# A gate multiplication two products later and two split remainders: moving VectorE work around a held gate-up pair

## The chip, the core and the metric

The kernel runs on one core of a Trainium2 chip. The metric is the device time of one execution in microseconds (us). Engines are named as the profile names them: PE is TensorE's matmul, PEld its weight load, DVE is VectorE, ACT is ScalarE, POOL is GpSimd, SP is SyncE, which issues DMAs.

## What is computed

A two-layer streaming encoder over 576 tokens (512 of a prompt and 64 of a sample) with width 1024. Each layer has two half-step SwiGLU feed-forward blocks (FFN), a mixer and a cross attention, each with a residual add. Only the FFN matters here:

```python
def swiglu(x, w_gu, w_down):
    gate, up = jnp.split(x @ w_gu, 2, axis=-1)
    return (jax.nn.silu(gate) * up) @ w_down
...
x = x + 0.5 * swiglu(rms_norm(x, ln_ffn1[l]), w_ffn1_gu[l], w_ffn1_down[l])
```

The hidden width is 2816, which is 22 tiles of 128. All values are fp32. A float32 product is made of three matmuls on rounded parts (high times high, high times low, low times high), so every operand needs a high part and a remainder.

## The kernel before

**Pairs and products.** Three of the four FFNs (the last one of layer 0 and both of layer 1) multiply by a scheme with seven products in place of eight. A *pair* is two weight tiles, gate and up of one hidden tile, or two output tiles of the down projection. Its seven products are numbered k = 0 to 6; `PLACE` says which of the three PSUM banks T, Y, W of the pair each goes to (k = 0, 3, 4, 6 to T, 1 and 5 to Y, 2 to W). Consecutive pairs alternate between two sets of banks. A product into a bank can start only when the epilogue of the product before it in that bank has been read out.

**Weights.** A weight piece arrives by DMA in `wraw` or `raw`. ACT casts it to the high part `wh` (`hi`, L149) and DVE subtracts to get the remainder `wl` (`lo`, L155). Both are made in program order about two to four products ahead of use. A sum of two pieces (`ss`, L319) is made by DVE and added to another piece by a DMA that POOL issues.

**Order of the work.** The program is a list of steps, one for each product. For each step the code first prepares weights (casts and remainders), then emits the matmuls, then calls the epilogue `pair_epi` (gate-up) or `down_epi` (down), and then `tick`, which runs what `defer(fn, n)` has put off: a function deferred by n in the epilogue of one step runs after the step n later. Each engine executes its own instructions in the order in which they were emitted.

**Parts and held pairs.** The 22 hidden tiles are worked in four parts of 6, 6, 4 and 6. Between the gate-up pairs of one part and its four down pairs D, E, ... stands one gate-up pair H of the next part. It is the *held* pair (`jj == 0 and not first`): its split hidden tile is kept back until the down pairs are done. There are three such places in each of the three FFNs, nine in all. The pair before H, the last gate-up pair of the part, is called G. Around the place the products run in this order:

```
... D.k0  H.k5  H.k4  D.k2  D.k1  H.k6  D.k3  E.k2  D.k5  D.k4 ...
```

The DVE epilogues are: H.k5, `ta` gets the second half of the gate (L599), then `gate` multiplies all of `ta` by the norm factor R (L594), and ACT's `silu` (L597) is put off; H.k4, `tc` from bank T (L610), which must be read before H.k6 may write T; H.k6, hidden = up times `ta` (L627 to L629, and L638 at six of the nine places); every down product, one L676 that adds its bank to X. D.k4 goes to the bank that the L676 of D.k3 reads. G's hidden tile is split into three operands: ACT makes the high parts, and `rest` makes the remainders: `hl<-td`, `qel<-hk` and a half-size `hl<-hk`. In the first two places of an FFN the down pairs work on six hidden tiles and their weight pieces are 384 wide (six *wide* places); in the third they work on four tiles and pieces are 256 wide (three *narrow* places).

Of the kernel before, what the change touches and what calls it, by code (L numbers as in the profile page):

```python
# [86 lines left out]
class Kernel:  # L87
# [471 lines left out]
    def ffn(self, gu, dn, gain_next, pairs=True, early=False):  # L559
# [4 lines left out]
        def pair_epi(k, pr, first, last, direct, early, late):  # L564

            T, Y, W = pr.banks
            tt = V.tensor_tensor
            jj = pr.jj
            one, two = slice(0, HF), slice(HF, NT)
            if k in (0, 2):  # L570
                if not pr.begun:
                    pr.begun = True
                    if first:
                        self.operand(st)
                        st["hk"] = self.fs["x"].tile([128, 3, HF], F32, tag="hk", name="hk")
                        for n in ("qeh", "qel"):
                            st[n] = self.fs["x"].tile([128, 2, 3, HF], F32R, tag=n, name=n)
                    pr.tb, pr.ta, pr.tc = (self.tmp(n) for n in ("tb", "ta", "tc"))
                    self.hi(pr.tb[:, one], (T, None, W)[k])
                else:  # L580
                    tt(pr.ta[:, one], (T, None, W)[k], pr.tb[:, one], op=ALU.add)  # L581
                    if last:
                        tt(pr.ta[:, one], pr.ta[:, one], st["R"][:, one], op=ALU.mult)
            elif k == 1:
                self.hi(pr.tb[:, two], Y)
            elif k == 3:
                self.hi(pr.tc[:, one], T)
                if first:
                    st["r"] = self.stats_tok(self.acc, self.ones, 1.0, ps=self.banks[:, 6:8])
                elif "R" not in st:  # L590
                    st["dg"] = self.diag(st["r"], "td")
            elif k == 5:
                def gate(c=slice(0, NT)):
                    tt(pr.ta[:, c], pr.ta[:, c], st["R"][:, c], op=ALU.mult)  # L594

                def silu():
                    nc.scalar.activation(pr.ta, pr.ta, AF.Silu)  # L597

                tt(pr.ta[:, two], Y, pr.tc[:, one], op=ALU.add)  # L599
                if first:  # L600
                    st["R"] = self.stats_bcast(None, dg=st.pop("dg"), ps=self.banks[:, 6:8])
                if last:
                    gate(two)
                    silu()
                    gate()
                else:
                    gate()
                    self.defer(silu, 3)
            elif k == 4:
                tt(pr.tc[:, two], T, pr.tb[:, two], op=ALU.add)  # L610
            else:
                qh, ql = st["qhh"], st["qhl"]
                kk = jj // 2
                hk = st["hk"]
                if direct or jj % 2:
                    h = self.tmp("td")
                else:
                    h = hk[:, 1:3].rearrange("p c n -> p (c n)")
                if last:
                    hh, hl = st["hh"][:, jj], st["hl"][:, jj]  # L620
                    for c, x in ((one, T), (two, pr.tc[:, two])):
                        tt(h[:, c], x, pr.ta[:, c], op=ALU.mult)
                        self.hi(hh[:, c], h[:, c])
                    for c in (one, two):
                        self.lo(hl[:, c], h[:, c], hh[:, c])
                    return
                tt(h[:, one], T, pr.ta[:, one], op=ALU.mult)  # L627
                tt(h[:, two], pr.tc[:, two], pr.ta[:, two], op=ALU.mult)
                tt(h, h, st["R"], op=ALU.mult)  # L629
                def sums():  # L630
                    tt(hk[:, 2], h[:, two], hk[:, 2], op=ALU.subtract)
                    V.scalar_tensor_tensor(hk[:, 1], hk[:, 2], -1.0, hk[:, 1], op0=ALU.mult, op1=ALU.subtract)
                    V.scalar_tensor_tensor(hk[:, 0], h[:, one], -1.0, hk[:, 1], op0=ALU.mult, op1=ALU.subtract)

                if direct:
                    parts = [(st["hh"][:, jj], st["hl"][:, jj], h)]
                elif jj % 2 == 0:
                    tt(hk[:, 0], hk[:, 1], hk[:, 2], op=ALU.subtract)  # L638
                    parts = [(qh[:, 0:2, kk], ql[:, 0:2, kk], hk[:, 0:2])]
                else:  # L640
                    parts = [(qh[:, 2:4, kk], ql[:, 2:4, kk], self.h2(h)),
                             (st["qeh"][:, :, kk], st["qel"][:, :, kk], hk[:, 1:3]),
                             (qh[:, 4, kk], ql[:, 4, kk], hk[:, 0])]

                def rest(ps):
                    for oh, ol, x in ps:
                        self.lo(ol, x, oh)

                def tail():
                    for oh, ol, x in parts:  # L650
                        self.hi(oh, x)
                    n = 0 if early or direct and late else 1
                    self.defer(lambda: rest(parts[:1]), n)
                    if parts[1:]:
                        self.defer(lambda: rest(parts[1:]), n + 1)

                if jj == 0 and not first:
                    st["held"] = tail
                elif direct and late:
                    tail()  # L660
                elif direct or jj % 2 == 0:
                    self.defer(tail, 1)
                elif early:
                    sums()
                    self.defer(tail, 1)
                else:
                    self.defer(lambda: (sums(), self.defer(tail, 0)), 1)
# [17 lines left out]
        def gate_up(j, jj, nj, direct):  # L685
            pr = Pair(gu[2 * j], gu[2 * j + 1],
                      lambda k, pr: pair_epi(k, pr, j == 0, direct and jj == nj - 1, direct, j == 0 or jj == nj - 1, jj == nj - 2), ops)
            pr.jj, pr.begun = jj, False
            seq.append(pr)
# [8 lines left out]
        parts = PARTS_S if pairs else PARTS  # L698
# [1813 lines left out]
```

## Time and profile before

| | before |
|---|---|
| device time, median of 3 runs | 2508.59 us (2506.38 to 2508.71) |
| the profiled execution, its own time | 2503.67 us |
| its span from first to last instruction | 2501.8 us |
| mean granted TensorE clock | 0.993 |
| PE busy | 2435.1 us, 97% |
| DVE busy | 1811.8 us, 72% |
| ACT busy | 1147.2 us, 46% |

The span lies 1.9 us inside the execution's own time, and that execution was 4.9 us faster than the median. Busy shares are means over the whole span: DVE at 72% has stretches in which it never rests. In a row of the trace, the part in brackets is how long the engine sat idle before the instruction and what ended that.

### The profile page before, as it was taken

What the parts mean: (1) busy time and instruction counts of PE and PEld (TensorE: products, weight loads), DVE (VectorE), ACT (ScalarE), POOL (GpSimd) and SP (SyncE); (2) the same over time, 40 slices, a digit from 0 to 9 for tenths busy, and PEclk for the clock granted to TensorE, in tenths of its full rate; (3) what the DMA queues carried; (4) which work ended last, traced back from release to release, by engine and by line L of the source; (5) the groups of instructions that cost most, each with busy time, mean ns of one, the idle gap of its engine ahead of it and who ended that gap; (6) DMA issues with size and microseconds to landing.
All of it is one profiled execution on the core that took longest, in us unless ns stands there. A gap on an engine that the chain in (4) does not pass through costs nothing.

```text
span 2501.8 us, 46574 instructions
## 1 busy us (share of the span) xinstructions
PE 2435.1 (97%) x18211; PEld 2391.6 (96%) x18211; DVE 1811.8 (72%) x3329; ACT 1147.2 (46%) x2093; POOL 617.3 (25%) x775
## 2 busy tenths in 40 slices
PE   8999999999999999999999999999999999999998
PEld 8998999999899999999999999999999999999998
DVE  6645658667875589898888888876753468989885
ACT  5222222334655465455556454452452355544554
POOL 1576135302320012222202222212310001222221
PEclk9999999999999999999999999999999999999999
DMA  4365653321134446766646767755972225676662
GB/s 157 91 189 186 154 129 116 120 96 37 37 107 134 131 118 148 169 156 160 150 112 147 169 142 179 158 148 174 295 250 86 84 94 135 144 181 150 155 144 76
DMA packets 160093, 350.87 MB, mean 140 GB/s; under 512 B 21585, under 2 KB 64257, under 8 KB 159233
## 3 DMA queue, kind: packets, MB, share of 16 engines
q1 hardware_dynamic: 115808, 277.09, 34.4%
q0 software_dynamic: 44064, 70.80, 18.1%
q8 instruction: 144, 2.36, 0.4%
q14 instruction: 77, 0.62, 0.1%
HBM read 292.26 MB, written 31.97 MB: 130 GB/s over the span
## 4 chain that ended last, share of the span: by engine, by line
PE 72%; DVE 12%; DMA 6%; ACT 3%; POOL 3%; issue 3%; SPq 1%; ACTq 0%; DVEq 0%; POOLq 0%
PE banks L349 34%; PE banks L428 27%; PE banks L2027 2%; DVE wl L236 2%; PE banks L772 1%; PE banks L1408 1%; PE banks L1376 1%; PE banks L1923 1%; PE banks L2303 1%; DVE wl L155 1%; DMA b<-in_ssm_bw 1%; ACT wh L149 1%; DMA f<-s5f 1%; DMA wraw<-ss 1%; DVE hl L155 1%
## 5 line engine op out<-in xcount | busy, mean ns | idle before, releaser
L149 ACT ACTIVATE wh<-wraw 128x512 fp32r<-128x512 f32 (+3 forms) x627 | 440.7, 719 | 339.6 <-PE banks L349 113.8
L236 DVE TENSOR_TENSOR wl<-wraw,wh 128x1024 fp32r<-128x1024 f32 (+2 forms) x216 | 262.5, 1220 | 153.3 <-ACT wh L149 151.0
L349 PE MATMUL banks<-xh,wh 128*128 128x288 f32 x1056 | 311.8, 295 | 1.6 <-ACT wh L149 1.3
L349 PE MATMUL banks<-xh,wl 128*128 128x288 f32 x1056 | 312.2, 296 | 1.0 <-DVE wl L155 0.9
L349 PE MATMUL banks<-xl,wh 128*128 128x288 f32 x1056 | 311.7, 295 | 0.0
L155 DVE TENSOR_TENSOR wl<-wraw,wh 128x512 fp32r<-128x512 f32 (+2 forms) x396 | 246.0, 627 | 59.3 <-ACT wh L149 58.2
L428 PE MATMUL banks<-xh,wh 128*128 128x288 f32 x1232 | 267.8, 299 | 9.0 <-ACT wh L149 8.1
L428 PE MATMUL banks<-xh,wl 128*128 128x288 f32 x1232 | 265.6, 297 | 4.2 <-DVE wl L236 4.2
L428 PE MATMUL banks<-xl,wh 128*128 128x288 f32 x1232 | 264.5, 297 | 0.0
L349 PE MATMUL banks<-eh,wh 128*128 128x288 f32 x792 | 236.9, 299 | 21.0 <-DVE tc L610 18.4
L349 PE MATMUL banks<-el,wh 128*128 128x288 f32 x792 | 234.5, 296 | 0.0
L349 PE MATMUL banks<-eh,wl 128*128 128x288 f32 x792 | 234.4, 296 | 0.0
L428 PE MATMUL banks<-hh,wh 128*128 128x288 f32 x1032 | 222.8, 297 | 3.6 <-ACT hh L149 1.8
L428 PE MATMUL banks<-hh,wl 128*128 128x288 f32 x1032 | 221.6, 296 | 3.3 <-DVE wl L236 3.3
L428 PE MATMUL banks<-hl,wh 128*128 128x288 f32 x1032 | 221.5, 296 | 0.5 <-DVE hl L155 0.5
L428 PEld LDWEIGHTS banks<-xh,wh 128*128 128x128 f32 x1232 | 199.5, 190 | 11.2 <-ACT wh L149 8.6
L428 PEld LDWEIGHTS banks<-xh,wl 128*128 128x128 f32 x1232 | 199.2, 190 | 5.5 <-DVE wl L236 5.4
L323 POOL DMA_DIRECT2D wraw<-ss x96 | 84.2, 885 | 473.8 <-DVE ta L581 217.7
L349 PEld LDWEIGHTS banks<-xh,wh 128*128 128x128 f32 x1056 | 199.0, 188 | 2.1 <-ACT wh L149 1.5
L349 PEld LDWEIGHTS banks<-xh,wl 128*128 128x128 f32 x1056 | 198.7, 188 | 1.5 <-DVE wl L155 1.5
L428 PEld LDWEIGHTS banks<-xl,wh 128*128 128x128 f32 x1232 | 199.4, 190 | 0.0
L349 PEld LDWEIGHTS banks<-xl,wh 128*128 128x128 f32 x1056 | 198.7, 188 | 0.0
(568 smaller groups left out, 6242.4 us busy)
## 6 DMA issues: line engine op xcount, KB each, us to landing
wraw<-in_gu SPq DMA_DIRECT2D x110, 512.0 KB
raw<-in_gu SPq DMA_DIRECT2D x66, 512.0 KB
wraw<-in_dn SPq DMA_DIRECT2D x56, 384.0 KB
raw<-in_gu POOLq DMA_DIRECT2D x66, 256.0 KB, 5.9
wraw<-in_gu POOLq DMA_DIRECT2D x66, 256.0 KB, 4.5
wraw<-ss POOLq DMA_DIRECT2D x66, 256.0 KB, 3.5
raw<-in_dn SPq DMA_DIRECT2D x24, 384.0 KB
wraw<-in_win SPq DMA_DIRECT2D x17, 512.0 KB
```

What stands on the lines that cost most here:

```text
L149: self.nc.scalar.activation(out, in_, AF.Copy)
L155: self.nc.vector.tensor_tensor(out, in_, hi.bitcast(F32), op=ALU.subtract)
L236: self.lo_engine.tensor_tensor(l[:p, :n], t[:p, :n], h[:p, :n].bitcast(F32), op=ALU.subtract)
L323: self.nc.gpsimd.dma_start(pr.r1[:, two], pr.src[3], accum_op=ALU.add)
L349: mm(out, ww[:, ws], xx[:, kk], start=k < 3 and kk == 0 and pi == 0, stop=kk == kn - 1 and pi == 2, skip_group_check=True)
L428: mm(ps[:M, h, :n], ww[:, k * M:(k + 1) * M], xx[:, k0 + k, h * n:(h + 1) * n], start=first and k == 0 and pi == 0, stop=last and k == kt ...
L772: nc.tensor.matmul(ps, ww[:, k * 128:(k + 1) * 128], xx[:, k, c0:c0 + n], start=k == 0 and pi == 0, stop=k == nj - 1 and pi == 2)
L1376: mm(out, x[:, k, t * 128:t * 128 + m], y[:, k], start=k == 0 and pi == 0, stop=k == 1 and pi == 2)
L1408: mm(out, x[:, k, f * 128:(f + 1) * 128], y[:, k, ts], start=k == 0 and pi == 0, stop=k == 1 and pi == 2)
L1923: mm(pv[:, m], x[:, kk, ms], y[:, k * MEM:(k + 1) * MEM], start=kk == m == pi == 0, stop=kk == 7 and pi == 2 and m == 1)
L2027: mm(ps[:, h, :HF], ww[:, k * 128:(k + 1) * 128], xx[:, k, h * HF:(h + 1) * HF], start=k == 0 and pi == 0, stop=k == 7 and pi == 2)
L2303: self.nc.tensor.matmul(out, ww[:, k * 128:(k + 1) * 128], xx[:, k], start=k == 0 and pi == 0, stop=k == KT - 1 and pi == 2)
```

## The change

For the held pair, `gate` is no longer emitted in the epilogue of H.k5: `gate` and `silu` together are deferred by two steps, so `gate` comes after D.k2 in place of H.k5 and `silu` after D.k2 in place of D.k1. For G (`early and not first`, with three operands), the second and third remainders come one and three products later.

```diff
                     gate(two)
                     silu()
                     gate()
+                elif jj == 0 and not first:
+                    self.defer(lambda: (gate(), silu()), 2)
                 else:
                     gate()
                     self.defer(silu, 3)
@@
                     for oh, ol, x in parts:
                         self.hi(oh, x)
                     n = 0 if early or direct and late else 1
-                    self.defer(lambda: rest(parts[:1]), n)
-                    if parts[1:]:
-                        self.defer(lambda: rest(parts[1:]), n + 1)
+                    for i, p in enumerate(parts):
+                        self.defer(lambda p=p: rest([p]), n + ((0, 2, 4) if early and not first else (0, 1, 1))[i])
```

The order of instructions changes on DVE and ACT alone; POOL's and SP's rows stay as they were but for buffer numbers. In the changed file the lines from 606 on move down by one or two: L610 becomes L612, L627 becomes L629, L676 becomes L677.

On DVE, at the first wide place, from behind L599 to H.k6's first epilogue instruction, before:

```order
L594 TENSOR_TENSOR ta<-ta,R 128x576
L155 TENSOR_TENSOR qel<-hk,qeh 128x2x288
L155 TENSOR_TENSOR hl<-hk,hh 128x288
L155 TENSOR_TENSOR wl<-ss,wh 128x384
L610 TENSOR_TENSOR tc<-banks,tb 128x288
L155 TENSOR_TENSOR wl<-wraw,wh 128x384
L319 TENSOR_TENSOR ss<-raw_10744,wraw 128x384
L676 SCALAR_TENSOR_TENSOR X<-banks,X 128x288
L155 TENSOR_TENSOR wl<-wraw,wh 128x384
L676 SCALAR_TENSOR_TENSOR X<-banks,X 128x288
L155 TENSOR_TENSOR wl<-wraw,wh 128x384
L627 TENSOR_TENSOR hk<-banks,ta 128x288
```

The same stretch in the changed kernel:

```order
L155 TENSOR_TENSOR wl<-ss,wh 128x384
L612 TENSOR_TENSOR tc<-banks,tb 128x288
L155 TENSOR_TENSOR qel<-hk,qeh 128x2x288
L155 TENSOR_TENSOR wl<-wraw,wh 128x384
L319 TENSOR_TENSOR ss<-raw_10744,wraw 128x384
L677 SCALAR_TENSOR_TENSOR X<-banks,X 128x288
L594 TENSOR_TENSOR ta<-ta,R 128x576
L155 TENSOR_TENSOR wl<-wraw,wh 128x384
L677 SCALAR_TENSOR_TENSOR X<-banks,X 128x288
L155 TENSOR_TENSOR hl<-hk,hh 128x288
L155 TENSOR_TENSOR wl<-wraw,wh 128x384
L629 TENSOR_TENSOR hk<-banks,ta 128x288
```

The same twelve instructions stand in both; `gate` (L594) and the two remainders have moved from ahead of H.k4's read-out to behind it. The three `wl<-wraw` rows are called A, B and C in what follows.

On ACT, at the same place, from the cast of the summed piece on, before:

```order
L149 ACTIVATE wh<-ss 128x384
L149 ACTIVATE wh<-wraw 128x384 x2
L597 ACTIVATE ta<-ta 128x576
L149 ACTIVATE wh<-wraw 128x384 x2
L149 ACTIVATE wh<-raw_10744 128x384
```

The same stretch in the changed kernel:

```order
L149 ACTIVATE wh<-ss 128x384
L149 ACTIVATE wh<-wraw 128x384
L597 ACTIVATE ta<-ta 128x576
L149 ACTIVATE wh<-wraw 128x384 x3
L149 ACTIVATE wh<-raw_10744 128x384
```

`silu` (L597) has moved ahead of one cast, the one for piece B; casts B and C now both stand behind it, and cast A stays ahead of it. At the narrow places it stands ahead of the casts of B and C in the same way.

## Rows read from the trace of the kernel before

**Rows 1.** The page, busy time of each engine over the span.

```profile
PE 2435.1 (97%) x18211; PEld 2391.6 (96%) x18211; DVE 1811.8 (72%) x3329; ACT 1147.2 (46%) x2093; POOL 617.3 (25%) x775
```

**Rows 2.** PE's waits: who waited <- for whom: us in total, times, longest.

```profile
PE banks L349 <- DVE tc L610: 18.4, 12, 2.3
```

**Rows 3.** Timeline of PE, first wide place: start, duration, what, [idle before].

```profile
1001.08 0.37 PE L349 MATMUL banks<-eh,wh 128*128 128x288 f32 x1 [1.55 <-DVE tc L610]
...
1006.08 0.29 PE L349 MATMUL banks<-hl,wh 128*128 128x288 f32 x1
1006.22 0.29 PE L349 MATMUL banks<-hh,wl 128*128 128x288 f32 x1
1006.53 0.38 PE L349 MATMUL banks<-qeh,wh 128*128 128x288 f32 x1
```

**Rows 4.** Timeline of DVE, first wide place.

```profile
997.82 0.45 DVE L599 TENSOR_TENSOR ta<-banks,tc 128x288 f32<-128x288 f32 x1
998.30 0.76 DVE L594 TENSOR_TENSOR ta<-ta,R 128x576 f32<-128x576 f32 x1
998.98 0.75 DVE L155 TENSOR_TENSOR qel<-hk,qeh 128x576 fp32r<-128x576 f32 x1
999.65 0.45 DVE L155 TENSOR_TENSOR hl<-hk,hh 128x288 fp32r<-128x288 f32 x1
1000.02 0.55 DVE L155 TENSOR_TENSOR wl<-ss,wh 128x384 fp32r<-128x384 f32 x1
1000.49 0.45 DVE L610 TENSOR_TENSOR tc<-banks,tb 128x288 f32<-128x288 f32 x1
1000.86 0.54 DVE L155 TENSOR_TENSOR wl<-wraw,wh 128x384 fp32r<-128x384 f32 x1
...
1001.79 0.44 DVE L676 SCALAR_TENSOR_TENSOR X<-banks,X 128x288 f32<-128x288 f32 x1
1002.16 0.54 DVE L155 TENSOR_TENSOR wl<-wraw,wh 128x384 fp32r<-128x384 f32 x1
...
1003.46 0.45 DVE L627 TENSOR_TENSOR hk<-banks,ta 128x288 f32<-128x288 f32 x1
...
1005.94 0.45 DVE L676 SCALAR_TENSOR_TENSOR X<-banks,X 128x288 f32<-128x288 f32 x1
```

**Rows 5.** Timeline of ACT, first wide place: casts B and C, with silu.

```profile
998.65 0.53 ACT L149 ACTIVATE wh<-wraw 128x384 fp32r<-128x384 f32 x1 [1.62 <-DMA wraw<-ss]
999.10 0.68 ACT L597 ACTIVATE ta<-ta 128x576 f32<-128x576 f32 x1
999.69 0.51 ACT L149 ACTIVATE wh<-wraw 128x384 fp32r<-128x384 f32 x1
```

**Rows 6.** Timeline of DVE, first narrow place.

```profile
1180.67 0.45 DVE L599 TENSOR_TENSOR ta<-banks,tc 128x288 f32<-128x288 f32 x1
...
1182.86 0.42 DVE L155 TENSOR_TENSOR wl<-ss,wh 128x256 fp32r<-128x256 f32 x1
1183.20 0.45 DVE L610 TENSOR_TENSOR tc<-banks,tb 128x288 f32<-128x288 f32 x1
...
1186.37 0.46 DVE L627 TENSOR_TENSOR td<-banks,ta 128x288 f32<-128x288 f32 x1 [0.66 <-PE banks L349]
...
1188.23 0.45 DVE L676 SCALAR_TENSOR_TENSOR X<-banks,X 128x288 f32<-128x288 f32 x1
```

**Rows 7.** Timelines of ACT and PE, first narrow place: cast C; H.k6.

```profile
1182.53 0.40 ACT L149 ACTIVATE wh<-wraw 128x256 fp32r<-128x256 f32 x1
1183.79 0.37 PE L349 MATMUL banks<-eh,wh 128*128 128x288 f32 x1 [2.26 <-DVE tc L610]
```

**Rows 8.** Windows H.k6 to D.k4, narrow places: span, engines' busy, granted clock, DMA.

```profile
1183.79:1189.38 5.59, 5.59 (x31) 5.59 (x31) 4.90 (x14) 1.45 (x4) 2.43 (x3) 0.69 0.34 47
1577.55:1581.88 4.33, 4.21 (x30) 4.00 (x31) 4.30 (x12) 1.45 (x4) 1.88 (x3) 1.00 0.35 45
2365.13:2370.72 5.59, 5.59 (x31) 5.59 (x31) 4.64 (x13) 1.45 (x4) 2.17 (x3) 0.69 0.33 47
```

## The prediction

> **What bounds the kernel now.** I read the page's busy times first: PE is busy for 97% of the span [rows 1], so a change is worth what it does to PE's waits. The list of PE's waits has one large entry inside the pair FFNs: twelve waits on H.k4's read-out L610, 18.4 us together [rows 2]. The timeline puts nine of them at H.k6 of the held pairs: six of about 1.55 us at the wide places, of which one stands in [rows 3], and three of about 2.27 us at the narrow ones, of which one stands in [rows 7]. That is 6 x 1.55 + 3 x 2.27 = 16.1 us, and what the change aims at. The other three, which share the remaining 2.3 us (0.77 each), belong to the last gate-up pair of each FFN, which it does not touch.
>
> Next I read what DVE does around such a wait [rows 4]. Behind L599 come the gate, `qel`, `hl`, a remainder, and only then L610. From L599 to the last row shown, the L676 that empties D.k3's bank, no row has a bracket: DVE does not rest for 8.12 us (997.82 to 1005.94). Then look at D.k4 in [rows 3]. Matmuls follow each other by about 0.13 us (1006.08, 1006.22), so D.k4 could have started at 1006.35. It started at 1006.53, when that L676 (1005.94, 0.45 long) had just ended. So at a wide place PE is held a second time, 5.45 us after the first, by the same unbroken DVE queue. What the place costs is set by when that L676 comes, not by L610.
>
> **The moved work on DVE.** The gate, `qel` and `hl` took 998.30 to 1000.02, 1.72 us, ahead of L610. They now come behind it. Nothing is added or removed: between L599 and L627 stand the same twelve instructions. From [rows 4], by distance between starts: a half-size operation such as L676 0.37 (1001.79 to 1002.16), gate 0.68, `qel` 0.67, a 384-wide remainder 0.47 (1000.02 to 1000.49), A and the sum behind it together 0.93 (1000.86 to 1001.79). The walk in the new order from L599 at 997.82: `wl<-ss` 998.19, L610 998.66, `qel` 999.03, A 999.70, L676 1000.63, gate 1001.00. L610 is 1.83 us earlier, more than PE's 1.55 us wait, so that wait closes. (L599 had 0.48 behind it because the gate reads what it writes; now 0.37, which is 0.1 gained.)
>
> If DVE kept going, remainder B would start at 1001.68, L627 at 1003.36 and the deciding L676 at 1005.84, 0.1 before its old time. PE would come to D.k4 early and wait there. The 1.55 us would be given back in full.
>
> **The moved work on ACT.** DVE does not keep going. `silu` needs the gate's result, and it now stands ahead of casts B and C. In before the gate ended at 999.06 and silu started at 999.10 [rows 4, 5]; now the gate ends at 1001.76, so silu starts at 1001.80. The next ACT instruction follows 0.59 after (999.10 to 999.69), so cast B, which ran at 998.65 in before, runs from 1002.39 to about 1002.90. Remainder B subtracts that cast; with the same 0.04 it starts at 1002.94 in place of 1001.68. DVE idles 1.26 us in a stretch that had no slack. Behind B are queued L676 of D.k1, `hl`, C, L627 to L638, and the deciding L676. On from 1002.94: L676 1003.41, `hl` 1003.78, C 1004.15 (its cast has ended by 1003.33), L627 1004.62 instead of 1003.46. From there the rows are unchanged: the deciding L676 at 1007.10, D.k4 at 1007.69. **A wide place ends 1.15 us later than before, six of them 6.9 us.**
>
> [...]
>
> **The narrow places.** The same walk with 256-wide pieces, whose remainder (and, I take it, sum) takes 0.34 (1182.86 to 1183.20), from L599 at 1180.67 [rows 6]: L610 1181.38, so H.k6 starts at 1181.97, 0.59 behind it as before (1183.20 to 1183.79); its wait falls from 2.26 to 0.44 us. `qel` 1181.75, A 1182.42, L676 1183.10, gate 1183.47 to 1184.23, silu 1184.27, cast B 1184.86 to 1185.26 (0.40 long [rows 7]), B 1185.30, L676 1185.64, `hl` 1186.01, C 1186.38, L627 1186.72 (before 1186.37, where DVE had waited 0.66 us for PE), the deciding L676 1.86 later at 1188.58, D.k4 at 1189.17 against 1189.38. That is 0.2 us gained. At the second narrow place PE was faster in before: D.k4 came 4.33 us after H.k6, not 5.59 [rows 8]. With the same distance from L599 to H.k6, the walk loses 5.59 - 4.33 - 0.2 = 1.05 us there; the third place is like the first. Three narrow places: 1.05 - 0.2 - 0.2, about **0.6 us lost**.
>
> **The clock.** The three windows of [rows 8] hold the same products, about thirty matmuls. [...] All three begin at the end of a wait of 2.3 us. So two of three such waits were followed by a stretch at the lower level. Thirty matmuls at 0.133 make 4.0 us and took 5.59; I take 1.5 us as the price of one such stretch. In the changed kernel PE waits longer, though at another product. Wide place: H.k6 starts where PE went idle in before (1001.08 - 1.55, less the 0.16 by which matmuls overlap: 999.37), 12 + 9 + 9 matmuls bring it to D.k5 at 1003.36, which waits for the L676 of D.k1 until 1004.00 (0.59 behind its start), and nine more to 1005.20; D.k4 starts at 1007.69. As the trace counts idle time that is about 0.5 and then 2.3 us. With two of three, four of the six wide places lose 1.5 us more: **6.0 us**. At a narrow place the same count gives about 0.9 and then 2.0 us. That lies between the 1.55 us waits, behind which the pace did not fall (12 + 3 x 9 = 39 matmuls in the 5.45 us from 1001.08 to 1006.53, 0.14 each [rows 3]), and the 2.3 us ones. I take half: 1.5 x 1.5 = **2.3 us**. The lower stretches of before are already in the D.k4 times above.
>
> **What is hidden.** Cast C ends 0.82 us before its remainder is due in the walk (1003.33 and 1004.15), and the casts behind it follow at once, since the buffers they wait for are free by then. If that cover were gone, each place would lose about one cast more (0.45, from 998.65 to 999.10 [rows 5]), 4 us in all. POOL's and SP's queues keep their order; their waits move with the buffers that DVE and PE release, and I cost them at nothing, since a piece is prepared at least two products ahead of its use (18 matmuls, 2.4 us) and everything behind D.k4 moves together. The 0.77 us waits stay.
>
> **Sum.** 6.9 + 0.6 + 6.0 + 2.3 = 15.8 us slower. The profiled execution took 2503.67, so it would take 2519.5; against the median of 2508.59, which is what runs are compared by, 2524.4.
>
> **Rivals.**
> First, *faster*: the wait at H.k6 goes and nothing takes its place. The gain is 16.1 less the 3 x 0.44 that remain, plus two lower stretches of 1.5 us: 17.8 us, 2490.8. For it speaks L610's 1.83 us; against it D.k4 of the wide places, which waited for DVE in before already. It decides for a gain of 5 us where the deciding L676 comes at least half a microsecond earlier than in before, and the walk finds 0.1 at best.
> Second, *the stall only moves*: the casts are not held up, DVE keeps going, and a wide place gains 0.1 us. A narrow one would have B at 1184.14, the deciding L676 at 1187.42 and D.k4 at 1188.01: 1.37 gained at the two places where the clock fell in before, 0.1 at the other. Together 3.4 us, 2505.2. PE's idle time at D.k4 would be 1.7 to 1.9 us, so up to three lower stretches may come back, 2509.7. It holds if silu's wait for the gate is covered, for which cast B has to end before 1001.68; against it, the order has B behind silu.
> Third, *slower with an undisturbed clock*: 6.9 + 0.6 = 7.5 us, 2516.1. And with a lower stretch at each of the nine places, 7.5 + 13.5 = 21.0 us, 2529.6.
>
> **How the numbers follow.** Forecast, slower with a lower clock at some to all of the nine places: 0.61. Slower with an undisturbed clock: 0.19. Stall only moves: 0.12. Faster: 0.08. About 0.2%, 5 us, is what a measurement of this kernel can tell from no change. So faster 0.08, same 0.12, slower 0.80. The range runs from 2512, where DVE's idle time at cast B is half of what I walked (3.5 us), to 2532, the nine lower stretches and the spread of the runs (2.3 us); the two cases below it hold 0.20.
>
> **What would show it.** In the changed profile PE's wait on `tc` shrinks to the three of 0.77 and three of about 0.4 us. In its place stand nine waits on L676 (now L677) at D.k4 of about 2.0 to 2.3 us, and shorter ones at D.k5. silu on ACT waits some 4.8 us for the gate, and DVE waits about 1.2 us on the cast behind it. Granted clock below 1 appears in the windows after D.k4. I am wrong if casts B and C end before DVE asks for them, if D.k4 starts no later after L599 than the 8.71 us of [rows 3, 4], or if the longer waits leave the clock alone.

## The result

| | before | after |
|---|---|---|
| device time, median | 2507.49 us (2505.55 to 2508.71, 4 runs) | 2523.64 us (2520.82 to 2525.86, 4 runs) |
| ratio of after to before | | 1.0065, 95% interval 1.0051 to 1.0079 |
| span of the profiled execution | 2501.8 us | 2524.1 us |

The changed kernel is 16.15 us slower by the medians; 2524.4 us was forecast.

The list of PE's waits after the change (who waited <- for whom: us in total, times, longest) answers to [rows 2]:

```profile
PE banks L349 <- DVE X L677: 24.0, 18, 2.3
...
PE banks L349 <- DVE tc L612: 3.6, 6, 0.8
```

The wait on H.k4's read-out has gone from 18.4 to 3.6 us: three waits of 0.77 us that the change does not touch, and three of 0.44 at the narrow places. The waits on X are now 24.0 us. Twelve of the eighteen are at D.k5 and D.k4 of the wide places and three at D.k4 of the narrow ones, 22.1 us together; the last three (1.14, 0.50 and 0.34 us) come 20 to 29 us behind the L599 of a narrow place. At D.k5 of the narrow places PE waits too, 0.81 us each, but the rows put this down to a cast on ACT, not to X.

The timeline of DVE at the first wide place (start, duration, what, [idle before]) answers to [rows 4]:

```profile
1001.84 0.45 DVE L599 TENSOR_TENSOR ta<-banks,tc 128x288 f32<-128x288 f32 x1
1002.20 0.55 DVE L155 TENSOR_TENSOR wl<-ss,wh 128x384 fp32r<-128x384 f32 x1
1002.67 0.45 DVE L612 TENSOR_TENSOR tc<-banks,tb 128x288 f32<-128x288 f32 x1
...
1005.00 0.76 DVE L594 TENSOR_TENSOR ta<-ta,R 128x576 f32<-128x576 f32 x1
1006.92 0.56 DVE L155 TENSOR_TENSOR wl<-wraw,wh 128x384 fp32r<-128x384 f32 x1 [1.16 <-ACT wh L149]
...
1008.60 0.45 DVE L629 TENSOR_TENSOR hk<-banks,ta 128x288 f32<-128x288 f32 x1
...
1011.09 0.45 DVE L677 SCALAR_TENSOR_TENSOR X<-banks,X 128x288 f32<-128x288 f32 x1
```

The read-out L612 comes 0.83 us behind L599 (2.67 in [rows 4]). Then there is a bracket in a stretch that had none: remainder B waited 1.16 us for its cast. The timeline of ACT there, which answers to [rows 5], shows what held the cast:

```profile
1005.79 0.69 ACT L597 ACTIVATE ta<-ta 128x576 f32<-128x576 f32 x1 [4.75 <-DVE ta L594]
1006.38 1.33 ACT L149 ACTIVATE wh<-wraw 128x384 fp32r<-128x384 f32 x3
```

ACT stood still for 4.75 us with silu at its head, and did three casts of `wraw` in one go once the gate had let silu through. The timeline of PE at the same place answers to [rows 3]; the first row is D.k5, the second D.k4:

```profile
1008.00 0.37 PE L349 MATMUL banks<-hh,wh 128*128 128x288 f32 x1 [0.47 <-DVE X L677]
...
1011.68 0.37 PE L349 MATMUL banks<-qeh,wh 128*128 128x288 f32 x1 [2.27 <-DVE X L677]
...
1012.37 0.44 PE L349 MATMUL banks<-qel,wh 128*128 128x288 f32 x1
1012.61 0.44 PE L349 MATMUL banks<-qeh,wl 128*128 128x288 f32 x1
```

D.k4 starts 9.84 us after L599, where it was 8.71 in before. All six wide places show 9.85. Behind the wait matmuls follow each other by 0.24 us instead of 0.13: the granted clock, 1.00 from L599 to D.k4, is 0.50 from 1012.5 to 1015.5. Windows of equal length from D.k4 on, at two wide places (span, busy of PE, PEld, DVE, ACT and POOL with their instruction counts, granted clock, DMA), show that this follows some of the waits and not others:

```profile
1011.68:1018.00 6.32, 6.32 (x36) 6.32 (x37) 5.24 (x12) 1.88 (x4) 2.50 (x3) 0.73 0.53 118
1518.99:1525.31 6.32, 6.32 (x48) 6.32 (x49) 5.96 (x15) 2.11 (x5) 2.52 (x3) 1.00 0.57 121
```

In 6.32 us PE got through 36 matmuls in the first and 48 in the second, though the waits ahead of them were both 2.26 to 2.27 us. Four of the six wide places look like the first (granted clock 0.73 three times and 0.53 once), two like the second (1.00).

What each place cost in the end is the distance from its L599 to the next place's. Windows of after, between wide and next place:

```profile
1001.84:1107.27 105.43, 102.65 (x758) 101.83 (x758) 89.92 (x176) 52.70 (x106) 26.29 (x30) 0.98 0.70 158
1402.57:1509.13 106.56, 103.76 (x758) 102.94 (x758) 89.83 (x175) 52.86 (x106) 26.26 (x30) 0.97 0.69 156
1509.13:1590.17 81.04, 78.27 (x587) 77.66 (x587) 68.50 (x137) 39.17 (x80) 21.07 (x24) 1.00 0.72 165
```

The same windows of before:

```profile
997.82:1100.76 102.94, 101.33 (x758) 100.38 (x758) 88.68 (x176) 52.73 (x106) 26.28 (x30) 1.00 0.71 162
1391.78:1494.53 102.75, 101.11 (x758) 100.28 (x758) 89.50 (x176) 53.13 (x106) 26.27 (x30) 1.00 0.72 162
1494.53:1574.42 79.89, 78.27 (x587) 77.65 (x587) 68.17 (x137) 39.37 (x80) 21.00 (x24) 1.00 0.72 167
```

The third pair differs by 1.15 us: this place, whose clock did not fall, cost what D.k4's delay cost (1.14) and nothing more. The first differs by 2.49, so the lower stretch, 3.4 us at 0.50, cost 1.35 more; the second by 3.81, with a stretch of twice the length (6.8 us at 0.50), 2.67 more.

A narrow place is not followed so closely by another, so there the windows run from D.k4 to the same later matmul, some 200 further on. The second and the third narrow place, in before:

```profile
1581.88:1611.22 29.34, 27.50 (x200) 26.69 (x201) 23.32 (x58) 13.16 (x32) 10.50 (x13) 1.00 0.74 149
2370.72:2399.74 29.02, 27.19 (x203) 26.59 (x202) 22.47 (x56) 12.60 (x30) 10.15 (x12) 1.00 0.68 146
```

The same two in after:

```profile
1598.62:1627.70 29.08, 28.57 (x200) 28.17 (x201) 24.99 (x59) 13.68 (x33) 11.29 (x13) 0.94 0.75 164
2393.09:2422.00 28.91, 28.55 (x200) 28.15 (x201) 24.40 (x59) 13.52 (x32) 10.83 (x13) 0.94 0.72 154
```

Both have a lower stretch in after and none in before, and yet they are 0.26 and 0.11 us shorter. PE is busy for over 1 us longer, but it stands idle for less: in before it waits on X again a little later, as in this row of the third place, and in after this wait is gone.

```profile
2383.32 0.37 PE L349 MATMUL banks<-qeh,wh 128*128 128x288 f32 x1 [1.30 <-DVE X L676]
```

So against before these two places are none the longer for their lower stretches. The first narrow place of after had none, and its window is 0.94 us longer than in before (28.44 for 27.50).

The two profiled spans differ by 22.3 us, more than the medians. Of this 4.0 us lie ahead of the first place (its L599 is at 1001.84 instead of 997.82), where the change reaches nothing; the profiled run of after is 2.2 us above its own median, and that of before 3.8 us below its own.

### The profile page after: what moved, and what is told of

Its sections match the earlier page's. It is cut to its first block, busy times and chain, and to the rows that moved or that the text cites. A ratio compares the mean times of both kernels' runs of the same rounds, so it can differ in the third digit from the quotient of the medians.

```text
span 2524.1 us, 46583 instructions
## 1 busy us (share of the span) xinstructions
PE 2449.0 (97%) x18211; PEld 2405.6 (95%) x18211; DVE 1814.6 (72%) x3329; ACT 1145.7 (45%) x2093; POOL 618.8 (25%) x775
## 4 chain that ended last, share of the span: by engine, by line
PE 75%; DVE 12%; DMA 5%; ACT 3%; POOL 2%; issue 2%; SPq 1%; ACTq 0%; DVEq 0%; POOLq 0%
PE banks L349 37%; PE banks L428 27%; DVE wl L236 1%; PE banks L2028 1%; PE banks L773 1%; PE banks L1409 1%; PE banks L1377 1%; PE banks L2304 1%; DVE wl L155 1%; DMA b<-in_ssm_bw 1%; PE banks L1924 1%; DMA f<-s5f 1%; DVE X L677 1%; DMA u<-s5u 1%; ACT wh L149 1%
```

## The experiments

The theory: in before, PE is held at a place twice by one unbroken DVE queue, and the second wait, on the deciding L676, sets what the place costs. So an earlier L610 gains nothing there, and the loss comes from silu, which waits for the late gate at the head of ACT's queue and keeps casts B and C from DVE. The rivals: the late gate or the late remainders cost by themselves, silu's new place costs by itself, or the first wait was worth its 1.55 us. The first four kernels ran together beside before at 2507.59 us (2502.12 to 2515.82, 29 runs), the other four beside before at 2507.25 us (2502.49 to 2513.81, 17 runs). Diffs are against the changed kernel unless it is said otherwise.

**The late gate, with silu behind cast B again.**

```diff
-                    self.defer(lambda: (gate(), silu()), 2)
+                    self.defer(gate, 2)
+                    self.defer(silu, 3)
```

> The changed kernel, with silu alone put back to three steps: the gate stays two products later and the remainders stay split, but on ACT silu stands behind cast B again. Theory (the late gate holds silu, and silu holds cast B, for which DVE rests 1.26 us): cast B is free, DVE has no bracket at remainder B, and D.k4 of a wide place starts about 8.6 us after L599 (before 8.71, changed 9.86); PE's wait only moves, to about 1.8 us at D.k4. Time of the kernel before less 3 us from the narrow places, plus up to nine lower clock stretches of 1.5 us at the moved wait: 2504 to 2514 us. Rival (the order of the gate and the remainders on DVE itself costs the time): D.k4 stays at about 9.86 us after L599 and the time at about 2523 us.

Measured: 2506.28 us (2501.23 to 2510.39, 12 runs), ratio 0.9988, interval 0.9977 to 0.9998. Cast B on ACT, the gate and remainder B on DVE, and D.k4 on PE, in the timelines of its first wide place (L599 at 1002.04):

```profile
1003.25 0.53 ACT L149 ACTIVATE wh<-wraw 128x384 fp32r<-128x384 f32 x1 [2.00 <-DMA wraw<-ss]
...
1005.21 0.75 DVE L594 TENSOR_TENSOR ta<-ta,R 128x576 f32<-128x576 f32 x1
1005.88 0.55 DVE L155 TENSOR_TENSOR wl<-wraw,wh 128x384 fp32r<-128x384 f32 x1
...
1010.68 0.37 PE L349 MATMUL banks<-qeh,wh 128*128 128x288 f32 x1 [1.76 <-DVE X L678]
```

Cast B runs 1.21 us behind L599, as soon as its data have landed (in after 4.54 us behind it, with silu ahead). Remainder B follows the gate by 0.67 us with no bracket, and D.k4 is 8.64 us behind L599. With the gate as late as in after, moving one activation back by one cast takes away the whole loss. PE still waits, for 1.76 us: the wait of 1.55 us at H.k6 has only moved to D.k4. This is the second rival of the prediction, made real, and its 2505.2 us is within 1.1 us of what was measured. Its price of up to three lower clock stretches did not show: windows of 6.32 us from D.k4 on at the first two wide places and the first narrow one have a granted clock of 1.00, and the whole profiled execution has 0.995.

**The gate's move alone**, with the old lines for the remainders:

```diff
-                    for i, p in enumerate(parts):
-                        self.defer(lambda p=p: rest([p]), n + ((0, 2, 4) if early and not first else (0, 1, 1))[i])
+                    self.defer(lambda: rest(parts[:1]), n)
+                    if parts[1:]:
+                        self.defer(lambda: rest(parts[1:]), n + 1)
```

> The change's first edit alone: gate and silu of the held pair two steps later, remainders as in the kernel before. Theory: silu is held as late as before the remainders' move allows, remainder B starts at most 0.4 us later than in the changed kernel but no half-size remainder follows it, so D.k4 of a wide place again starts about 9.86 us after L599 and the time is that of the changed kernel, 2518 to 2527 us; the wait at H.k6 is about 0.9 us. Rival (the split remainders cost the time): as the kernel before, 2505 to 2509 us.

Measured: 2521.18 us (2517.51 to 2524.83, 6 runs), ratio 1.0046, interval 1.0030 to 1.0062. H.k6 and D.k4 in the timeline of PE at its first wide place (L599 at 1001.89):

```profile
1004.36 0.38 PE L349 MATMUL banks<-eh,wh 128*128 128x288 f32 x1 [0.76 <-DVE tc L612]
...
1011.73 0.37 PE L349 MATMUL banks<-qeh,wh 128*128 128x288 f32 x1 [1.89 <-DVE X L678]
```

D.k4 is 9.84 us behind L599, as in after, with remainder B 1.16 us late again. The place is split differently: 0.76 us of waiting at H.k6 and 1.89 at D.k4. The gate's move alone loses 13.6 us, most of the change's 16.15, and the two intervals overlap; the remainders decide where PE stands.

**The remainders' move alone**, without the gate's branch:

```diff
-                elif jj == 0 and not first:
-                    self.defer(lambda: (gate(), silu()), 2)
```

> The change's second edit alone: the second and third remainder one and three products later, gate and silu as in the kernel before. Theory: L610 comes 1.04 us earlier and the wait at H.k6 falls to about 0.5 us, but DVE does the same work up to the deciding L676, so D.k4 of a wide place starts 8.71 us after L599 as before and PE waits about 1 us there: no gain at wide places; up to 3 us gained where the clock fell at two narrow places: 2503 to 2508 us. Rival (the split remainders cost the time): 2518 us and more. Rival (closing the wait at H.k6 is worth its length): 2507.5 less 9 x 1.04, 2498 us.

Measured: 2506.96 us (2502.08 to 2511.01, 12 runs), ratio 0.9986, interval 0.9976 to 0.9996. H.k6 and D.k4 in the timeline of PE at its first wide place (L599 at 1002.42):

```profile
1004.64 0.37 PE L349 MATMUL banks<-eh,wh 128*128 128x288 f32 x1 [0.51 <-DVE tc L610]
...
1011.13 0.37 PE L349 MATMUL banks<-qeh,wh 128*128 128x288 f32 x1 [1.08 <-DVE X L675]
```

The first wait fell by 1.04 us and a second one of 1.08 us came: D.k4 is 8.71 us behind L599, exactly as in [rows 3, 4]. Closing two thirds of the first wait was worth nothing at this wide place. At the narrow places D.k4 is at 7.43 instead of 8.71, 7.46 and 8.72, 2.6 us over three, but 200 matmuls behind D.k4 only 0.5 us of this is left. The median gained 0.6 us.

**silu ahead of cast B, with the gate early:**

```diff
-                    self.defer(lambda: (gate(), silu()), 2)
+                    gate()
+                    self.defer(silu, 2)
```

> The changed kernel with the gate back in the epilogue of H.k5, silu two steps later: on ACT silu stands ahead of casts B and C as in the changed kernel, but its gate is early; the remainders stay split. Theory (silu ahead of the casts costs something only because its gate comes late): no bracket at remainder B, D.k4 of a wide place 8.7 us after L599, the time that of the remainders' edit alone, 2503 to 2508 us. Rival (silu's place ahead of casts B and C costs the time whenever the gate comes): casts B and C are late, 2518 us and more.

Measured: 2506.05 us (2502.12 to 2515.72, 12 runs), ratio 0.9995, interval 0.9983 to 1.0006. silu on ACT, remainder B on DVE and D.k4 on PE in the timelines of its first wide place (L599 at 1003.13):

```profile
1004.41 0.68 ACT L597 ACTIVATE ta<-ta 128x576 f32<-128x576 f32 x1 [2.07 <-DVE ta L594]
...
1007.10 0.55 DVE L155 TENSOR_TENSOR wl<-wraw,wh 128x384 fp32r<-128x384 f32 x1
...
1011.85 0.37 PE L349 MATMUL banks<-qeh,wh 128*128 128x288 f32 x1 [1.08 <-DVE X L678]
```

silu stands in after's place on ACT, but waits 2.07 us instead of 4.75, DVE has no bracket at B, and D.k4 is 8.72 us behind L599 (7.42 at the narrow places). Its new place is harmless by itself: only together with the late gate does it cost.

**Less DVE work ahead of the deciding L676.** If the whole queue between L599 and that L676 sets the place, taking work out of it should gain what an earlier L610 could not. The scaling of the held pair's hidden tile (L629 of before, and L638 at the wide places) is not needed before the down pairs are done, so it is put off by six products, on top of the first experiment:

```diff
-                tt(h, h, st["R"], op=ALU.mult)
+                held = jj == 0 and not first
+                if not held:
+                    tt(h, h, st["R"], op=ALU.mult)
...
-                    tt(hk[:, 0], hk[:, 1], hk[:, 2], op=ALU.subtract)
+                    if not held:
+                        tt(hk[:, 0], hk[:, 1], hk[:, 2], op=ALU.subtract)
...
+                    def scale():
+                        tt(h, h, st["R"], op=ALU.mult)
+                        if not direct:
+                            tt(hk[:, 0], hk[:, 1], hk[:, 2], op=ALU.subtract)
+                    self.defer(scale, 6)
```

> The kernel with silu behind cast B, and for the held pair alone the product with R (L629) and the difference (L638) six steps later, behind the deciding L676; nothing needs them before the down pairs end. Theory (the place costs what DVE has to do between L599 and the deciding L676): that work shrinks by 1.27 us, D.k4 of a wide place starts about 7.4 us after L599 (silu behind B alone 8.64, before 8.71), PE's one wait there falls from 1.76 to about 0.5 us, and the time to 2493 to 2500 us. Rival (DVE meets the postponed work a little later and PE waits there instead): D.k4 early but a new wait behind it of about the same size, 2505 us and more.

Measured: 2499.52 us (2492.45 to 2500.87, 6 runs), ratio 0.9960, interval 0.9948 to 0.9972. D.k4 in the timeline of PE at its first wide place (L599 at 1000.59):

```profile
1007.96 0.37 PE L349 MATMUL banks<-qeh,wh 128*128 128x288 f32 x1 [0.47 <-DVE X L687]
```

D.k4 comes 7.36 us behind L599, 1.35 earlier than in before, and 6.59 at the narrow places. Over the nine places that is 6 x 1.35 + (24.89 - 3 x 6.59) = 13.2 us; the median gained 7.7. In the profiled execution most of it stayed: 200 matmuls behind D.k4 the nine places together are still 12.3 us ahead of before, and the span is 2490.6 us for 2501.8. But that execution is the fastest of the six, 4.9 us and more below the others, which left no trace, so why the median gained less stays open.

**The same late scaling in the old order**, without the change:

> The kernel before with the same two instructions of the held pair six steps later and nothing else. Theory (two waits in a row on one DVE queue, of which the first hides the second): the wait at H.k6 stays at 1.55 us and sets D.k4, which can come only 0.18 us earlier at a wide place, 8.53 us after L599; 2504 to 2507.5 us. Rival (each part of the shorter DVE work is worth its length): 1.27 us at six places, 2500 us or less.

Measured: 2505.69 us (2500.11 to 2512.32, 11 runs), ratio 0.9994, interval 0.9984 to 1.0005. H.k6 and D.k4 in the timeline of PE at its first wide place (L599 at 1000.11):

```profile
1003.37 0.37 PE L349 MATMUL banks<-eh,wh 128*128 128x288 f32 x1 [1.56 <-DVE tc L610]
...
1008.64 0.29 PE L349 MATMUL banks<-qeh,wh 128*128 128x288 f32 x1
```

Now D.k4 has no wait and starts 8.53 us behind L599, 0.18 earlier than before: the same edit that is worth 1.3 us a place behind the first one is worth 0.18 here, because H.k6's wait binds instead. This is the other half of the theory: of these two waits in a row, either alone was worth almost nothing at a wide place (0.00 and 0.18 us).

**Two further steps on the late scaling.** The next kernel adds to the kernel with silu behind cast B and the late scaling: the third remainder comes four products later still.

```diff
-                        self.defer(lambda p=p: rest([p]), n + ((0, 2, 4) if early and not first else (0, 1, 1))[i])
+                        self.defer(lambda p=p: rest([p]), n + ((0, 2, 8) if early and not first else (0, 1, 1))[i])
```

> The kernel with silu behind cast B and the late scaling, and the third remainder another four products later, also behind the deciding L676: 0.37 us less for DVE. Theory (ACT holds again): silu ends too late for cast C, remainder C has to wait about 0.4 us for it, D.k4 stays at about 7.4 us after L599 and the time within 1.5 us of the kernel with the late scaling. Rival (DVE's work alone counts): D.k4 at 7.0 us, 2 us faster than that kernel.

Measured: 2495.77 us (2493.28 to 2500.74, 5 runs), ratio 0.9948, interval 0.9935 to 0.9961. Remainder C on DVE in the timeline of its first wide place (L599 at 1002.27):

```profile
1007.36 0.56 DVE L155 TENSOR_TENSOR wl<-wraw,wh 128x384 fp32r<-128x384 f32 x1 [0.33 <-ACT wh L149]
```

D.k4 stayed at 7.36 behind L599: the time that the remainder left free became an idle 0.33 us of DVE ahead of remainder C, whose cast is still behind silu. The median is 3.75 us under that of the kernel above, where 1.5 was allowed for, though the place is no shorter; the two intervals overlap, and the runs don't say whether the difference is real.

The last kernel changes this one once more: the gate comes one product later than in before instead of two.

```diff
-                    self.defer(gate, 2)
+                    self.defer(gate, 1)
```

> As the kernel before this one (late scaling, third remainder late), with the gate of the held pair one product later in place of two, still behind L610; silu as there. Theory (a gate that comes 2 us earlier frees ACT): no bracket at remainders B and C, D.k4 of a wide place about 7.0 us after L599, 0.4 us earlier than in the kernel with the gate two later, L610 as early and no wait at H.k6; 2 to 3 us faster than it, 2490 to 2497 us. Rival (the gate ahead of A delays A and with it PE): a wait on a remainder at D.k2 or E.k2, no gain over it.

Measured: 2496.24 us (2495.63 to 2500.99, 5 runs), ratio 0.9955, interval 0.9943 to 0.9967. D.k4 came 6.94 us behind L599 (6.14 at the narrow places), with 0.05 us of waiting left there at the wide ones and none at their H.k6. That is 0.42 us earlier than in the kernel above at six places and 0.45 at three, 3.9 us, but no gain showed in the time, where 2 to 3 us were expected. The timelines of DVE and PE, in the down pairs behind its first narrow place, show part of it given back:

```profile
1204.46 0.42 DVE L155 TENSOR_TENSOR wl<-raw,wh 128x256 fp32r<-128x256 f32 x1 [1.97 <-ACT wh L149]
1204.81 0.45 DVE L687 SCALAR_TENSOR_TENSOR X<-banks,X 128x288 f32<-128x288 f32 x1
...
1206.37 0.37 PE L349 MATMUL banks<-qeh,wh 128*128 128x288 f32 x1 [1.03 <-DVE X L687]
```

Here DVE waits for a cast, and PE for DVE, some 27 us behind L599. In the kernel above the same two waits are 1.52 and 0.56 us, so this narrow place gives back the 0.45 us that it gained. But 200 matmuls behind D.k4 the three narrow places have lost only 1.1 us of the 3.9 in this way and the wide ones nothing; where the rest went stays open, with five runs of each kernel.

## Why the prediction was right

**What bounds the kernel.** Right: the wait at H.k6 closed (18.4 to 3.6 us) and gained nothing at the wide places. The experiments show the reason given, two waits in series on one queue: the remainders alone closed two thirds of the first wait with D.k4 unmoved at 8.71, and the late scaling alone closed the second for 0.18.

**The walk on DVE and ACT.** It gave D.k4 at 9.87 us behind L599 at a wide place; 9.85 was measured, at all six. By distance between starts remainder B was 1.92 us behind the gate (1005.00 to 1006.92), 1.94 in the walk. At D.k5 and D.k4 the waits were 0.46 to 0.48 and 2.25 to 2.27, for 0.5 and 2.3. At the narrow places D.k4 was to be at 8.50 and was at 8.45 in all three, with waits of 0.44, 0.81 and 1.89 for 0.44, 0.9 and 2.0. So the wide places lost 6 x 1.14 = 6.8 us (forecast 6.9), and the narrow ones 3 x 8.45 - 24.89 = 0.5 (forecast 0.6). By its own rows the walk's 1.15 for a wide place is 1.16. One reading was off: at D.k5 of a narrow place PE was to wait for the L676 of D.k1, but in after the row of the first one names a cast:

```profile
1195.40 0.37 PE L349 MATMUL banks<-hh,wh 128*128 128x288 f32 x1 [0.81 <-ACT wh L149]
```

There silu held up a cast that PE itself was waiting for. The L677 of D.k1 had ended 0.1 us before that cast did (1195.25 and 1195.35), so it made hardly a difference.

**The cast behind silu.** The step on which the sign rested. The first experiment shows that silu's place ahead of cast B is necessary for the loss, the one with the early gate that it is not sufficient, and the gate alone that the two together are. That a cast whose data have landed stays behind a waiting silu was the author's assumption from the order of the instructions, and no row of before shows it. In after it can be seen: the transfer that cast B needs was issued at 999.60 and landed 3.0 us later, but silu waited 4.75 us at the head, and the three casts behind it were done in one go from 1006.38; without silu ahead, in the first experiment, cast B ran 1.21 us behind L599 instead of 4.54.

**The clock.** What the prediction calls the lower level is a granted clock of 0.50 in the traces, at the two narrow places of before (1185.5 to 1187.5 and 2366 to 2369) as in after. The count was right at the wide places (four of six) and half a place low at the narrow ones (two of three, for 1.5). The rate of two in three had been read off three places, so that it fitted so well in one execution is in part luck; the four runs of after have mean granted clocks of 0.988 to 0.991, so the count need not be the same in all. By the distances between places the four wide stretches cost 1.35, 1.56, 2.67 and 1.51 us, 7.1 together for 6.0; one of them was of double length, which the prediction had not allowed for.

The term of the sum that was mis-sized is the 2.3 us for the clock at the narrow places. Behind D.k4 these lost 0.94, -0.26 and -0.11 us by the windows above, 0.6 together, and the two with a lower stretch are the two that lost nothing: a later wait on X (1.30 us at the third place), which is gone in after, made room for it. The prediction let everything behind D.k4 move together and did not look at the waits that follow there.

So the terms come to 6.8 + 0.5 + 7.1 + 0.6 = 15.0 us in this execution, for a forecast of 15.8 and beside 16.15 between the medians. The clock was 1.1 too low at the wide places and 1.7 too high at the narrow ones, so the sum came nearer than its terms, which is luck too. With the 4.0 us ahead of the first place, 3.3 of the 22.3 between the profiled spans are left for what lies between and behind the places. That the lower stretches, and not only D.k4's delay, belong to the loss at the wide places follows from the windows above; the three kernels of the first four that lost nothing have mean granted clocks of 0.994 and 0.995 in the profiled execution, where after has 0.988.

**The rivals.** *Faster* failed where the prediction said: the deciding L676 did not come earlier. *The stall only moves* is the first experiment. *Slower with an undisturbed clock* (2516.1) lies below all four runs.

## What to carry to other kernels

When one engine is held twice by the same unbroken queue of another, read the price of the place from the last instruction that it waits for, and walk that queue in the new order before moving anything: here, with the remainders moved alone, the first wait fell from 1.55 to 0.51 us and a second one of 1.08 us came. When a producer is put off, look at what stands behind its consumer on the next engine, and leave the consumer behind the work that is ready before it: here silu at the head of ACT's queue waited 4.75 us, and three casts came behind it. The change put the gate off by two products and moved silu ahead of a cast, and the two together made the loss. To shorten such a place, take work out from ahead of the last wait: put off what nobody needs yet, here the scaling of a held tile, which with silu behind cast B and the moved remainders made the kernel 0.4 to 0.5% faster than before.

## What the runs showed of the hardware

Whether a wait of PE was followed by a stretch at a granted clock of 0.50 was not settled by its length alone. These are the mean granted clocks of windows behind the waits at the held pairs' places in the profiled executions, 6.32 us from D.k4 on, and from H.k6 to D.k4 where the wait is at H.k6; 1.00 is a window without a lower stretch:

| wait | where | granted clock behind it |
|---|---|---|
| 2.25 to 2.27 us, after 0.46 to 0.48 at D.k5 | after, D.k4, wide | 0.73, 0.73, 0.53, 1.00, 1.00, 0.73 |
| 2.26 to 2.27 us | before, H.k6, narrow | 0.69, 1.00, 0.69 |
| 1.89 us, after 0.81 at D.k5 | after, D.k4, narrow | 1.00, 0.73, 0.73 |
| 1.89 us, after 0.76 at H.k6 | gate alone, D.k4, first two wide | 1.00, 0.73 |
| 1.9 us at most | silu behind cast B, D.k4, first narrow | 1.00 |
| 1.76 us | silu behind cast B, D.k4, first two wide | 1.00, 1.00 |
| 1.54 to 1.56 us | before, H.k6, wide | 1.00 at all six |

Waits of the same length went differently: behind those of 2.25 to 2.27 us a lower stretch came at six of nine places, behind those of 1.89 us at three of the five read, and behind the six of 1.54 to 1.56 us at none. What decided it at a place the runs don't tell: no experiment changed the earlier wait alone.

What such a stretch cost differed too. Behind the wide places of after one cost 1.35 to 1.56 us, and one of double length 2.67; behind two narrow places of after, where PE in before had waited on X again, the window that held the stretch came out at 29.08 and 28.91 us, for 29.34 and 29.02 in before.
